# Placing all matrix operands of a two-block network at one place modulo 256 bytes

## The chip, the cores and the metric

The kernel runs on one core of a Trainium2 chip. The metric is the device time of one execution in microseconds (us), as the median of several runs. Of one further execution the hardware profiler kept a trace; all rows below come from it.

## What is computed

The input is 256 rows of 1024 numbers in float32. Two blocks follow each other: `first_block` has two layers, `second_block` four SwiGLU feed-forward parts, one hybrid mixer and one recurrent mixer. Cut to the matrix products, which carry the work:

```python
def first_block(x, ...):                       # layers "first0", "first1"
    for l in range(2):
        h = rms_norm(x, norm_g[l])
        ... = split(h @ w_in[l])               # gmlp, retention, gated delta net (GDN)
        branches = stack([y_a, y_b, y_c])
        gates = sigmoid(einsum(h, w_gate[l]))
        x = x + sum(gates * einsum(branches, w_branch_out[l])) @ w_out[l]
    return rms_norm(x, final_norm_g)

def second_block(x, ...):                      # ffn00, hyb, ffn01, ffn10, rec, ffn11
    for layer in range(2):
        h = swiglu(rms_norm_2(x, g[0]), ffn_w_in[layer, 0], ffn_w_out[layer, 0])
        x = x + 0.5 * rms_norm_2(h, g[1])
        h = rms_norm_2(x, g[2])
        h = hybrid_mixer(h, ...) if layer == 0 else recurrent_mixer(h, ...)
        x = x + rms_norm_2(h, g[3])
        h = swiglu(rms_norm_2(x, g[4]), ffn_w_in[layer, 1], ffn_w_out[layer, 1])
        x = x + 0.5 * rms_norm_2(h, g[5])
    return x
```

## The kernel before

**Products in three passes.** Each float32 operand is split into a high part and a low part in the type fp32r (`split`: ScalarE casts, VectorE subtracts), and a product is the sum of high x high, high x low and low x high. The normalised rows stand transposed in `hh` and `hl`; the hidden values of a feed-forward part in `ah` and `al`; other left operands are `yh`/`yl`, `g2` (printed as `g`), `oh`/`ol`, `roh`/`rol`.

**Weight units.** `unit` fetches the next 128 x 1024 piece of the weight stream into `st` by a DMA and splits it into `wh` and `wl`. Six buffers of each lie in the pool `wp`. In the feed-forward parts and the recurrent mixer three more lie in the pool of the phase (`xp`); there, of each nine units that follow each other, six use the first pool and three the second.

**Three loops use the units.** A matmul has a stationary operand (128 x 128, loaded by LDWEIGHTS while the matmul ahead of it runs) and a moving operand. In a trace row `mm<-a,b`, a is the moving operand and b the stationary one.
- `ws`: the unit is stationary and `hh`/`hl` move (256 columns). A unit takes 24 matmuls, in the order `hh,wh`, `hl,wh`, `hh,wl`. There are 208 such units: 36 in each of the four feed-forward parts, 24 in the two layers of the first block, 28 in the hybrid mixer, 12 in the recurrent one.
- `xs` and `outp`: the unit moves (512 columns) and the left operand is stationary; a unit takes 12 matmuls. `outp` of a feed-forward part uses 22 units.

**Where operands lie.** A tile gets its address from the order and the sizes of the tiles in its pool. In the program as built, modulo 256 bytes: `hh`, `hl` and the units of `wp` start at 128; the units of `xp` at 192 in the feed-forward parts and at 160 in the recurrent mixer; `ah`/`al` and `g2` at 192, `oh`/`ol` at 64, `roh`/`rol` at 160, `yh`/`yl` at 0. Slices step by multiples of 512 bytes, so a whole tile has one place. Below, the **offset** of a pair is the place of the stationary operand that is loaded during a matmul, less the place of that matmul's moving operand, modulo 256. By the program, the `ws` matmuls stand so: offset 0 for 156 units (96 of them in the feed-forward parts), 64 for the 48 units of `xp` in the feed-forward parts, 32 for 4 units of the recurrent mixer. In `outp` of the feed-forward parts 60 units have offset 64 and 28 have 0; `outp` of the first block (`g2`, 16 units) has 64, that of the hybrid mixer (`oh`, 16 units) 192. The 24 units on `yh` have 128, some 8 on `roh` 32, the 8 on `hh` that use `xp` 192. All other `xs` units, on `hh`, have 0.

**Order.** Instructions of PE, DVE, ACT and the SP queue are put in order by a scheduler; POOL follows the program. `step` runs one piece of background work (GDN, retention, LRU, attention) between the parts of a loop.

Of the kernel before, what the change touches and what calls it, by code (L numbers as in the profile page):

```python
# [23 lines left out]
FX = 2  # L24

NW, NS = 6, 5

LO, LF, LH, LR = 4, 6, 4, 5

# [139 lines left out]
class Net:  # L169
# [36 lines left out]
        return self.ps.tile([128, 512], F32, tag="mm", name="mm", bufs=4)  # L206

    def t(self, tag, shape, dt=F32, bufs=1, pool=None):
        return (pool or self.ph).tile([128] + list(shape), dt, tag=tag, name=tag, bufs=bufs)

    def bcast(self, row, tag, c0=0, n=1024):
        t = self.t(tag, [n])
# [65 lines left out]
        self.nc.scalar.copy(hi, src)  # L278
        self.nc.vector.tensor_sub(lo, src, hi)  # L279

    def unit(self, g=None):

        if self.pre:
            return self.pre.popleft()
        st = self.wp.tile([128, 1024], F32, tag="st", name="st", bufs=NS)
        self.nc.sync.dma_start(st, self.a["wst"][self.wi])
        pool, n = self.wp, NW
        if self.ui % (NW + self.xn) >= NW:
            pool, n = self.xp, self.xn
        self.wi += 1  # L290
        self.ui += 1
        hi = pool.tile([128, 1024], F32R, tag="wh", name="wh", bufs=n)
        lo = pool.tile([128, 1024], F32R, tag="wl", name="wl", bufs=n)
        if g is None:
            self.split(hi, lo, st)
        else:
            for j in range(2):
                s = self.pn[:, g + j:g + j + 1]
                self.act(hi[:, CS[j]], st[:, CS[j]], AF.Copy, scale=s)
                self.stt(lo[:, CS[j]], st[:, CS[j]], s, hi[:, CS[j]], MUL, SUB)  # L300
        return hi, lo
# [57 lines left out]
    def ws(self, evac, pair=None):  # L359

        self.flush()
        hh, hl = self.hT
        ps = [self.mmt().rearrange("p (a b) -> p a b", a=2) for _ in range(2)]
        for k2 in range(4):
            wh, wl = (w.rearrange("p (a b) -> p a b", a=2) for w in self.unit(None if self.gn is None else self.gn + 2 * k2))
            for f in range(4):
                p = ps[f // 2][:, f % 2]  # L370
                fs = slice(f * 128, f * 128 + 128)
                for j in range(2):
                    k = k2 * 2 + j
                    self.mm(p, wh[:, j, fs], hh[:, :, k], start=k == 0 and f % 2 == 0, stop=False)
                    self.mm(p, wh[:, j, fs], hl[:, :, k], start=False, stop=False)
                    self.mm(p, wl[:, j, fs], hh[:, :, k], start=False, stop=k == 7 and f % 2 == 1)
                if f % 2:
                    if k2 == 3 and pair is not None:
                        pair(f // 2, ps[f // 2])
                    elif k2 == 3:  # L380
                        for e in (f - 1, f):
                            evac(e, ps[e // 2][:, e % 2])
                    self.step()
# [2 lines left out]
        hh, hl = self.hT  # L386
        return lambda k, t: (hh[:, t, k], hl[:, t, k])

    def small_proj(self, src, n, out):

        w = self.t("junk", [512], pool=self.sp)[:, :8 * n].rearrange("p (a b) -> p a b", a=8)
        self.nc.sync.dma_start(w, src.rearrange("p (a b) -> p a b", a=8))
        wh, wl = self.t("spwh", [8, n], F32R), self.t("spwl", [8, n], F32R)
        self.split(wh, wl, w)
        hh, hl = self.hT
        yield
        p = self.sm()[:n, :256]
        for k in range(8):
            self.mm(p, wh[:, k], hh[:, :, k], start=k == 0, stop=False)
            self.mm(p, wh[:, k], hl[:, :, k], start=False, stop=False)  # L400
            self.mm(p, wl[:, k], hh[:, :, k], start=False, stop=k == 7)
            if k % 2:
                yield
        o = self.t("junk", [512], pool=self.sp)[:, :256]
        self.nc.scalar.copy(o[:n], p)
        yield
        p = self.sm()[:, : 2 * n].rearrange("p (a b) -> p a b", a=2)
        for t in range(2):
            self.nc.tensor.transpose(p[:, t], o[:n, TS[t]], self.ident[:n, :n])
        out.append(p)  # L410
# [75 lines left out]
    def post(self, ph, half, prep, tag="h"):  # L486

        g = self.bcast(B_PN + POST[ph], "bcp")  # L490
        k = 4.0 if half else 1.0
        rs = self.rs

        tmps, vs = [None, None], [None, None]

        def cb(t, c, ps):
            if c == 0:
                tmps[t] = self.t(tag, [1024], bufs=2)
                vs[t] = self.t("rsv", [1], bufs=4, pool=self.sp)
            tmp, v = tmps[t], vs[t]  # L500
            ss = self.sumsq(ps, self.t("junk", [512], pool=self.sp))
            self.tt(tmp[:, CS[c]], ps, g[:, CS[c]])
            if c == 0:
                self.ts(v, ss, k / D, rs[t][:, 1:2] if half else EPS, MUL, ADD)
                return
            self.stt(v, ss, k / D, v, MUL, ADD)
            r = self.t("rsr", [1], bufs=4, pool=self.sp)
            self.pw(r, v)
            for c in range(2):
                x = self.x[t][:, CS[c]]  # L510
                self.stt(x, tmp[:, CS[c]], r, x, MUL, ADD)
            prep(t, tmp)

        return cb
# [26 lines left out]
    def run(self):  # L541
        tc, nc, a = self.tc, self.nc, self.a
        with (
# [22 lines left out]

            self.act(cp.tile([128, 1], F32, tag="first", name="first"), self.mhalf[:, :1], AF.Tanh)
            nc.sync.dma_start(self.x[0], a["x"][TS[0]])
            with tc.tile_pool(name="start", bufs=1) as self.ph:
                prep = self.prep_open(self.phases[0])  # L570
                nc.sync.dma_start(ci, a["ci"])
                nc.sync.dma_start(self.x[1], a["x"][TS[1]])

                z, warm = self.t("z", [128]), self.sm()
                nc.vector.memset(z, 0.0)
                for n in range(WARM):
                    self.mm(warm[:, :128], z, z, start=True, stop=True)
                self.ui = self.xn = 0
                for t in range(2):
                    prep(t, self.t("h", [1024], bufs=2))  # L580
                    if t == 0 and self.phases[0].startswith("first"):
                        first = [self.unit() for _ in range(3)]
                self.pre.extend(first)
# [3 lines left out]
            for p in order:  # L587
                i = self.phases.index(p) + 1
                nxt = self.phases[i] if i < len(self.phases) else None
                self.hT, self.rs = self.next  # L590
                self.gn = PN.get(p)
                self.ui = 0
                self.xn = 0 if p.startswith("first") or p == "hyb" else 3
                with tc.tile_pool(name=p, bufs=1) as self.ph:
                    self.xp = self.ph if self.xn else None
                    if p.startswith("first"):
                        self.first(int(p[5]), nxt)
                    elif p.startswith("ffn"):
                        self.ffn(p, nxt)
                    elif p == "hyb":  # L600
                        self.hyb(nxt)
                    elif p == "rec":
                        self.rec(nxt)
                    self.flush()
# [345 lines left out]
    def gdn_ab(self, l, G):  # L950
        nc = self.nc
        ab = []
        yield from self.small_proj(self.a["sw"][:, S_AB + l * 128:S_AB + (l + 1) * 128], 16, ab)
        ab = ab[0]
        sv = self.sv[:, l * V_L:(l + 1) * V_L]
        ar = self.t("gar", [8])
        self.act(ar, sv[:, 8:16], AF.Exp)
        xa = self.t("gxa", [2, 2, 4])
        be = self.t("gbe", [2, 2, 4])
        for t in range(2):  # L960
            a4 = ab[:, t].rearrange("p (d w h) -> p d w h", d=2, w=2)
            self.tt(xa[:, t], a4[:, :, 0], sv[:, 16:24].rearrange("p (d h) -> p d h", d=2), ADD)
            self.act(be[:, t], a4[:, :, 1], AF.Tanh, scale=0.5)
        xf = xa.rearrange("p t d h -> p (t d h)")
        g = self.t("gg", [2, 2, 4])
        gf = g.rearrange("p t d h -> p (t d h)")
        self.softplus(gf, xf, [16], "gs")
        for t in range(2):
            gt = g[:, t].rearrange("p d h -> p (d h)")
            self.stt(gt, gt, -1.0, ar)  # L970
        bf = be.rearrange("p t d h -> p (t d h)")
        nc.vector.tensor_scalar(bf, bf, 0.5, 0.5, op0=MUL, op1=ADD)
        G.update(g=g, be=be)

    def gdn_core(self, G):
# [87 lines left out]
        ea, eb = [ex[:, 0], ex[:, 2]], [ex[:, 1], ex[:, 3]]  # L1063
        for _ in range(5):
            yield
        tx = self.t("gtx", [256])[:64]
        for j in range(1, 31):
            n = 31 - j
            u = tx[:, :n * j].rearrange("p (a b) -> p a b", a=n)
# [155 lines left out]
    def hyb(self, nxt):  # L1225
# [29 lines left out]
        def gate(g):  # L1255

            def cz(t, ps):
                th = self.silu2(ps, "h2", 5)
                yv = y[t][:, g * 8:g * 8 + 8].rearrange("p a b -> p (a b)")
                self.tt(yv, yv, th)  # L1260
                junk = self.t("junk", [512], pool=self.sp)
                r = self.rstd(self.sumsq(yv, junk), 1.0 / 512, 4 * EPS)
                self.stt(yv, yv, r, gb[:, CS[g]])
                ks = slice(4 + g * 8, 8 + g * 8)
# [293 lines left out]
```

## Time and profile before

| what | value |
|---|---|
| median of 3 runs | 1722.13 us (1720.92 to 1723.18) |
| profiled execution, its own time | 1723.59 us |
| its span in the trace | 1721.6 us |
| mean granted TensorE clock | 0.992 |
| PE busy (share of the span) | 1690.0 us (98%) |
| DVE, ACT, POOL busy | 1193.8, 883.7, 154.3 us |

The span is the time from the first to the last instruction in the trace; 2.0 us of the execution's time lie around it. A matmul's busy time is longer than the distance to the next one, since matmuls are pipelined: the distance between starts (the pitch) is what a matmul costs.

### The profile page before, as it was taken

The page shows a single profiled execution, that of the slowest core. Times are in us where ns is not written, and L with a number is a line of the kernel's source. Part 1 is how long each engine was busy: PE and PEld are TensorE (multiplying, and loading weights), DVE is VectorE, ACT ScalarE, POOL GpSimd, SP SyncE. Part 2 cuts the span into 40 slices and gives each one's busy share as a digit, 9 for nine tenths or more (in the row PEclk, how much of TensorE's full clock was granted, in tenths as well). Part 3 has the DMA queues.
Part 4 walks back from the last instruction along what each step waited for, and adds up shares of the span by engine and source line. Part 5 has one row for each costly group of instructions (what it writes and reads, how often), then busy time and mean ns, then how long its engine had stood idle before and what let it go on. Part 6 is the DMA issues. An engine that isn't in the chain of part 4 may idle for free.

```text
span 1721.6 us, 26744 instructions
## 1 busy us (share of the span) xinstructions
PE 1690.0 (98%) x10312; PEld 1493.2 (87%) x10312; DVE 1193.8 (69%) x1941; ACT 883.7 (51%) x1387; POOL 154.3 (9%) x205
## 2 busy tenths in 40 slices
PE   9999999999999999999999999999999999999998
PEld 8888888798878888998798887999789987879986
DVE  6888666679855658764678767775586637987743
ACT  5553344554523447553554556653475435875532
POOL 0157000004630000000000000000000000000000
PEclk9999999999989999999999999999999999999999
DMA  8546435554553447554454335754565545446542
GB/s 292 171 163 208 135 105 195 175 175 154 171 171 111 160 156 257 186 184 149 164 171 156 106 128 195 237 185 149 177 242 187 184 151 201 162 150 227 178 156 73
DMA packets 83279, 296.80 MB, mean 172 GB/s; under 512 B 9680, under 2 KB 10320, under 8 KB 83152
## 3 DMA queue, kind: packets, MB, share of 16 engines
q1 hardware_dynamic: 81360, 289.85, 51.0%
q0 software_dynamic: 1792, 5.24, 1.1%
q8 instruction: 81, 1.33, 0.3%
q14 instruction: 46, 0.38, 0.1%
HBM read 290.33 MB, written 4.72 MB: 171 GB/s over the span
## 4 chain that ended last, share of the span: by engine, by line
PE 81%; DVE 7%; POOL 4%; ACT 3%; DMA 2%; issue 2%; SPq 0%; POOLq 0%; DVEq 0%; ACTq 0%
PE mm L199 71%; PE gd L199 6%; PE sm L199 2%; PE sm L274 2%; DVE wl L279 2%; POOL rsr L417 1%; POOL gtx L1070 1%; POOL gv L1072 1%; DMA st<-in_wst_dram 1%; DVE wl L193 1%; ACT wh L278 1%; PE gd L274 1%; DVE x L193 1%; DVE ro L190 1%; ACT wh L196 1%
## 5 line engine op out<-in xcount | busy, mean ns | idle before, releaser
L279 DVE TENSOR_TENSOR wl<-st,wh 128x1024 fp32r<-128x1024 f32 x348 | 429.2, 1241 | 278.6 <-ACT wh L278 277.5
L278 ACT CAST wh<-st 128x1024 fp32r<-128x1024 f32 x348 | 364.0, 1049 | 439.5 <-PE mm L199 402.4
L199 PE MATMUL mm<-hh,wh 128*128 128x256 f32 x1664 | 474.9, 285 | 0.0
L199 PE MATMUL mm<-hl,wh 128*128 128x256 f32 x1664 | 471.9, 284 | 0.0
L199 PE MATMUL mm<-hh,wl 128*128 128x256 f32 x1664 | 471.2, 283 | 0.0
L199 PEld LDWEIGHTS mm<-hh,wh 128*128 128x128 f32 x1664 | 318.9, 192 | 2.4 <-issue 1.7
L199 PEld LDWEIGHTS mm<-hl,wh 128*128 128x128 f32 x1664 | 317.4, 191 | 2.1 <-issue 1.7
L199 PEld LDWEIGHTS mm<-hh,wl 128*128 128x128 f32 x1664 | 317.4, 191 | 1.2 <-issue 1.0
L193 DVE SCALAR_TENSOR_TENSOR wl<-st,ci,wh 128x512 fp32r<-128x512 f32 x352 | 251.3, 748 | 77.5 <-ACT wh L196 77.5
L196 ACT ACTIVATE wh<-st,ci 128x512 fp32r<-128x512 f32 x352 | 233.9, 715 | 105.2 <-PE mm L199 81.1
L199 PE MATMUL mm<-wh,hh 128*128 128x512 f32 x656 | 267.8, 410 | 2.3 <-ACT wh L278 2.3
L199 PE MATMUL mm<-wh,hl 128*128 128x512 f32 x656 | 260.4, 397 | 0.0
L199 PE MATMUL mm<-wl,hh 128*128 128x512 f32 x656 | 259.0, 396 | 0.0
L199 PEld LDWEIGHTS mm<-wh,hh 128*128 128x128 f32 x656 | 124.9, 190 | 26.6 <-ACT wh L278 2.5
L199 PEld LDWEIGHTS mm<-wh,hl 128*128 128x128 f32 x656 | 124.5, 190 | 26.7 <-issue 0.5
L199 PEld LDWEIGHTS mm<-wl,hh 128*128 128x128 f32 x656 | 124.9, 190 | 24.2 <-issue 0.5
L199 PE MATMUL mm<-wl,ah 128*128 128x512 f32 x352 | 138.9, 394 | 0.0
L199 PE MATMUL mm<-wh,ah 128*128 128x512 f32 x352 | 138.4, 393 | 0.0
L199 PE MATMUL mm<-wh,al 128*128 128x512 f32 x352 | 138.3, 393 | 0.0
L417 POOL TENSOR_TENSOR rsr<-rsv,mhalf 128x1 f32<-128x1 f32 (+1 forms) x32 | 28.9, 902 | 1207.9 <-DVE rsv L193 940.0
L199 PEld LDWEIGHTS mm<-wh,ah 128*128 128x128 f32 x352 | 65.9, 187 | 15.8
L199 PEld LDWEIGHTS mm<-wh,al 128*128 128x128 f32 x352 | 65.9, 187 | 15.6
(385 smaller groups left out, 2019.6 us busy)
## 6 DMA issues: line engine op xcount, KB each, us to landing
st<-in_wst_dram SPq DMA_DIRECT2D x524, 512.0 KB, 4.0
bcp<-in_bc_dram SPq DMA_DIRECT2D x7, 512.0 KB, 5.4
gdl<-g POOLq DMA_DIRECT2D x8, 256.0 KB, 2.7
cst<-in_bc_dram SPq DMA_DIRECT2D x4, 512.0 KB, 5.2
g<-gdt POOLq DMA_DIRECT2D x8, 256.0 KB, 4.4
bcn<-in_bc_dram SPq DMA_DIRECT2D x3, 512.0 KB, 5.2
x<-in_x_dram SPq DMA_DIRECT2D x2, 512.0 KB, 4.8
cst<-in_cst_dram SPq DMA_DIRECT2D x4, 256.0 KB, 4.1
```

Source lines behind the costliest of these rows:

```text
L190: self.nc.vector.tensor_scalar(o, a, s1, s2, op0=op0, op1=op1)
L193: self.nc.vector.scalar_tensor_tensor(o, a, s, b, op0=op0, op1=op1)
L196: self.nc.scalar.activation(o, i, f, **k)
L199: self.nc.tensor.matmul(*a, **k)
L274: self.nc.tensor.transpose(p[:, j], s, self.ident)
L278: self.nc.scalar.copy(hi, src)
L279: self.nc.vector.tensor_sub(lo, src, hi)
L417: self.nc.gpsimd.tensor_tensor(o, i, self.mhalf[:, :i.free_size()], op=ALU.pow)
L1070: nc.gpsimd.tensor_tensor(u, X[:, j + 1:, j:j + 1].to_broadcast([64, n, j]), X[:, j:j + 1, :j].to_broadcast([64, n, j]), op=MUL)
L1072: nc.gpsimd.tensor_tensor(X[:, j + 1:, :j], X[:, j + 1:, :j], u, op=SUB)
```

## The change

Four things are done. `unit` allocates one tile of 2112 elements, which holds the high part and, 4096 bytes further, the low part, and takes an offset for each: `ws` asks for 16 and 48 elements (64 and 192 bytes), the other loops for none. Small tiles, whose size isn't a multiple of 256 bytes, go to a pool of their own (`phs`) behind that of the phase, and `junk` is lengthened, so that all tiles of the other pools start at the same place. `small_proj` keeps its split weights for GDN in the buffers of `yh`/`yl` (two of each) and not in `spwh`/`spwl`, and the POOL solve of GDN keeps its products `tx` in one of the two `ggm` buffers and not in `gtx`.

```diff
+WS = 16, 48
...
     def t(self, tag, shape, dt=F32, bufs=1, pool=None):
-        return (pool or self.ph).tile([128] + list(shape), dt, tag=tag, name=tag, bufs=bufs)
+        pool = pool or (self.phs if math.prod(shape) % 64 else self.ph)
+        return pool.tile([128] + list(shape), dt, tag=tag, name=tag, bufs=bufs)
...
-    def unit(self, g=None):
+    def unit(self, g=None, off=(0, 0)):
...
-        hi = pool.tile([128, 1024], F32R, tag="wh", name="wh", bufs=n)
-        lo = pool.tile([128, 1024], F32R, tag="wl", name="wl", bufs=n)
+        w = pool.tile([128, 2112], F32R, tag="wh", name="wh", bufs=n)
+        hi, lo = (w[:, a + o:a + o + 1024] for a, o in zip((0, 1024), off))
...
-            wh, wl = (w.rearrange("p (a b) -> p a b", a=2) for w in self.unit(None if self.gn is None else self.gn + 2 * k2))
+            wh, wl = (w.rearrange("p (a b) -> p a b", a=2) for w in self.unit(None if self.gn is None else self.gn + 2 * k2, WS))
...
-        wh, wl = self.t("spwh", [8, n], F32R), self.t("spwl", [8, n], F32R)
+        wh, wl = (self.t(g, [512], F32R, bufs)[:, :8 * n].rearrange("p (a b) -> p a b", a=8) for g in tags)
...
-        yield from self.small_proj(self.a["sw"][:, S_AB + l * 128:S_AB + (l + 1) * 128], 16, ab)
+        yield from self.small_proj(self.a["sw"][:, S_AB + l * 128:S_AB + (l + 1) * 128], 16, ab, ("yh", "yl"), 2)
...
-        tx = self.t("gtx", [256])[:64]
+        tx = self.t("ggm", [256], bufs=2)[:64]
```

In the program as built, `hh`, `hl`, `ah`, `al`, `g2`, `yh`, `oh`, `roh` and the units of `xs` and `outp` then start at 128 modulo 256, so that all their matmuls have offset 0 but seven. In `ws` the high part starts at 192 (offset 64) and the low part at 64 (offset 192). The order `hh,wh`, `hl,wh`, `hh,wl` makes that offsets 64, 192, 64: during `hh,wh` the same high part is loaded anew, during `hl,wh` the low part, during `hh,wl` the next high part. Every engine runs the same instructions as before, and each feed-forward part in the same order; the order differs in places of the other phases.

One place is on DVE in `first0`, where units of `ws` are subtracted while GDN's gates (`gxa`, `gsu`, `gss`) are computed; names of semaphores that an instruction waits for stand in brackets. Before:

```order
L184 TENSOR_TENSOR gxa<-sm,sv 128x8 [waits Activation_49]
L193 SCALAR_TENSOR_TENSOR gsu<-gxa 128x16 [waits DVE_49]
L279 TENSOR_TENSOR wl<-st,wh 128x1024 [waits DMAHW2_49,PE_49,Activation_49]
L193 SCALAR_TENSOR_TENSOR g_266<-mm,pp,g_266 128x255 [waits Activation_49]
L188 TENSOR_SCALAR gss<-gsu 128x16 [waits Activation_49]
```

And of the change, at the same place on DVE:

```order
L186 TENSOR_TENSOR gxa<-sm,sv 128x8 [waits Activation_49]
L195 SCALAR_TENSOR_TENSOR g_270<-mm,pp,g_270 128x255 [waits Activation_49]
L195 SCALAR_TENSOR_TENSOR gsu<-gxa 128x16 [waits DVE_49]
L195 SCALAR_TENSOR_TENSOR g_270<-mm,pp,g_270 128x255 [waits DVE_49]
L283 TENSOR_TENSOR wh<-st,wh 128x1024 [waits DMAHW2_49,Activation_49]
```

The subtraction no longer waits for PE itself, only for the cast, since the cast ahead of it now writes into a tile that both parts share and waits until PE has read both; the low part is now printed as `wh` too.

The other place is on PE in `rec`, where the last `ws` matmuls end, `outp` begins (`mm<-wh,roh`) and the last two gate matmuls of the LRU (`rx,wa` and `rx,wx`) stand between them. Before:

```order
L199 MATMUL mm<-hh,wh 128x256
L199 MATMUL mm<-hl,wh 128x256
L199 MATMUL mm<-hh,wl 128x256
L199 MATMUL mm<-wh,roh 128x512
L199 MATMUL mm<-wl,roh 128x512
L199 MATMUL mm<-wh,rol 128x512
L199 MATMUL gd<-rx_14238,wa 128x256
L199 MATMUL gd<-rx_14238,wx 128x256
L199 MATMUL mm<-wh,roh 128x512
```

And of the change:

```order
L201 MATMUL mm<-hh,wh 128x256 x2
L201 MATMUL mm<-hl,wh 128x256
L201 MATMUL gd<-rx_13831,wa 128x256
L201 MATMUL gd<-rx_13831,wx 128x256
L201 MATMUL mm<-hh,wh 128x256
L201 MATMUL mm<-wh,roh 128x512 x2
L201 MATMUL mm<-wh,rol 128x512
```

The two gate matmuls have moved from behind the first three matmuls of `outp` to ahead of them.

## Rows read from the trace of the kernel before

**Rows 1.** The page: span, and PE's busy time with its share and instructions.

```profile
span 1721.6 us, 26744 instructions
...
PE 1690.0 (98%) x10312; PEld 1493.2 (87%) x10312; DVE 1193.8 (69%) x1941; ACT 883.7 (51%) x1387; POOL 154.3 (9%) x205
```

**Rows 2.** The page: the chain that ended last, by engine.

```profile
PE 81%; DVE 7%; POOL 4%; ACT 3%; DMA 2%; issue 2%; SPq 0%; POOLq 0%; DVEq 0%; ACTq 0%
```

**Rows 3.** Waits of PE: for what, us in total, times, longest.

```profile
PE gd L199 <- DVE g L1100: 7.7, 3, 3.7
...
PE mm L199 <- ACT roh L278: 2.8, 1, 2.8
PE mm L199 <- ACT wh L278: 2.3, 1, 2.3
```

**Rows 4.** The page's groups: count, busy us, mean ns of one, idle before.

```profile
L199 PE MATMUL mm<-hh,wh 128*128 128x256 f32 x1664 | 474.9, 285 | 0.0
...
L193 DVE SCALAR_TENSOR_TENSOR wl<-st,ci,wh 128x512 fp32r<-128x512 f32 x352 | 251.3, 748 | 77.5 <-ACT wh L196 77.5
L196 ACT ACTIVATE wh<-st,ci 128x512 fp32r<-128x512 f32 x352 | 233.9, 715 | 105.2 <-PE mm L199 81.1
...
L199 PE MATMUL mm<-wl,ah 128*128 128x512 f32 x352 | 138.9, 394 | 0.0
```

**Rows 5.** Timeline of PE, ffn00, first `ws` unit (`xp`): start us, us.

```profile
673.96 0.61 PE L199 MATMUL sm<-rdg,cst 128*128 128x128 f32 x4
...
674.76 0.28 PE L199 MATMUL mm<-hh,wh 128*128 128x256 f32 x1
...
676.91 0.28 PE L199 MATMUL mm<-hl,wh 128*128 128x256 f32 x1
```

**Rows 6.** Timeline of PE, the next six `ws` units (`wp`).

```profile
677.14 0.38 PE L274 MATMUL sm<-ci,sg 128*128 128x128 f32 x2
...
677.84 0.28 PE L199 MATMUL mm<-hl,wh 128*128 128x256 f32 x1
...
693.92 0.28 PE L199 MATMUL mm<-hh,wh 128*128 128x256 f32 x1
```

**Rows 7.** Timeline of PE, the three `ws` units behind them (`xp`).

```profile
694.75 0.28 PE L199 MATMUL mm<-hl,wh 128*128 128x256 f32 x1
...
702.76 0.28 PE L199 MATMUL mm<-hh,wh 128*128 128x256 f32 x1
```

**Rows 8.** Timeline of PE, `xs` on `hh` in first0, offset 0.

```profile
127.75 0.39 PE L199 MATMUL mm<-wh,hh 128*128 128x512 f32 x1
...
136.82 0.39 PE L199 MATMUL mm<-wl,hh 128*128 128x512 f32 x1
```

**Rows 9.** Timeline of PE, `outp` of ffn00, units at offset 64.

```profile
779.65 0.39 PE L199 MATMUL mm<-wh,ah 128*128 128x512 f32 x1
...
786.89 0.39 PE L199 MATMUL mm<-wl,ah 128*128 128x512 f32 x1
```

**Rows 10.** Timeline of PE, `outp` of the hybrid mixer, offset 192.

```profile
1032.79 0.39 PE L199 MATMUL mm<-wh,oh 128*128 128x512 f32 x1
...
1043.77 0.39 PE L199 MATMUL mm<-wh,oh 128*128 128x512 f32 x1
```

**Rows 11.** Timeline of PE, `ws` of the recurrent mixer, offset 32.

```profile
1464.76 0.28 PE L199 MATMUL mm<-hh,wl 128*128 128x256 f32 x1
...
1468.90 0.28 PE L199 MATMUL mm<-hl,wh 128*128 128x256 f32 x1
```

**Rows 12.** Waits of ACT: the cast of a unit.

```profile
ACT wh L278 <- PE mm L199: 402.4, 227, 8.8
```

**Rows 13.** Timeline of PE, the last gate matmuls of the LRU.

```profile
1497.77 0.59 PE L199 MATMUL gd<-rx,wa 128*128 128x256 f32 x2
```

**Rows 14.** Tile `ggm` in first0 (first and last start), and POOL's first product.

```profile
L199 PE MATMUL gd<-ggm,cst x8: 591/592/676, 66.6 to 82.4; 128*128 128x512 f32 x8
...
98.59 0.35 POOL L1070 TENSOR_TENSOR gtx<-gv 64x30 f32<-64x30 f32 x1 [3.51 <-DMA gv<-gdl]
```

More of the change, by code (lines that the diff above doesn't have):

```diff
@@ L387, in hlhs, with small_proj @@
         return lambda k, t: (hh[:, t, k], hl[:, t, k])
-    def small_proj(self, src, n, out):
-        w = self.t("junk", [512], pool=self.sp)[:, :8 * n].rearrange("p (a b) -> p a b", a=8)
+    def small_proj(self, src, n, out, tags=("spwh", "spwl"), bufs=1):
+        w = self.t("junk", [560], pool=self.sp)[:, :512][:, :8 * n].rearrange("p (a b) -> p a b", a=8)
         self.nc.sync.dma_start(w, src.rearrange("p (a b) -> p a b", a=8))
-        wh, wl = self.t("spwh", [8, n], F32R), self.t("spwl", [8, n], F32R)
+        wh, wl = (self.t(g, [512], F32R, bufs)[:, :8 * n].rearrange("p (a b) -> p a b", a=8) for g in tags)
         self.split(wh, wl, w)
@@ L403, in small_proj @@
                 yield
-        o = self.t("junk", [512], pool=self.sp)[:, :256]
+        o = self.t("junk", [560], pool=self.sp)[:, :512][:, :256]
         self.nc.scalar.copy(o[:n], p)
@@ L500, in cb @@
             tmp, v = tmps[t], vs[t]
-            ss = self.sumsq(ps, self.t("junk", [512], pool=self.sp))
+            ss = self.sumsq(ps, self.t("junk", [560], pool=self.sp)[:, :512])
             self.tt(tmp[:, CS[c]], ps, g[:, CS[c]])
@@ L568, in run @@
             nc.sync.dma_start(self.x[0], a["x"][TS[0]])
-            with tc.tile_pool(name="start", bufs=1) as self.ph:
+            with tc.tile_pool(name="start", bufs=1) as self.ph, tc.tile_pool(name="starts", bufs=1) as self.phs:
                 prep = self.prep_open(self.phases[0])
@@ L593, in run @@
                 self.xn = 0 if p.startswith("first") or p == "hyb" else 3
-                with tc.tile_pool(name=p, bufs=1) as self.ph:
+                with tc.tile_pool(name=p, bufs=1) as self.ph, tc.tile_pool(name=p + "s", bufs=1) as self.phs:
                     self.xp = self.ph if self.xn else None
@@ L1260, in cz @@
                 self.tt(yv, yv, th)
-                junk = self.t("junk", [512], pool=self.sp)
+                junk = self.t("junk", [560], pool=self.sp)[:, :512]
                 r = self.rstd(self.sumsq(yv, junk), 1.0 / 512, 4 * EPS)
```

## The prediction

> **What bounds the kernel now.** I read the page first: PE is busy for 1690.0 of 1721.6 us, 98% [rows 1], and the chain that ended last is 81% PE, with 7% DVE and 4% POOL [rows 2]. Then the waits of PE: the largest is 7.7 us in three pieces for GDN's `g`, then 2.8 us once for `roh` and 2.3 us once for a `wh` [rows 3]. So almost nothing is late for PE, and time can come only from matmuls that follow each other faster. The groups give no cost per matmul: 285 ns is the mean busy time of an `hh,wh` and 394 ns that of a `wl,ah` [rows 4], but matmuls overlap. So I went to the timeline and took distances between starts, over long stretches without a break.
>
> The reader should see two things there. First, one `ws` loop runs at three speeds. The first unit of ffn00 lies in `xp` (offset 64) and takes (676.91 − 674.76)/19 steps = 113.2 ns per matmul [rows 5]; the next six lie in `wp` (offset 0): (693.92 − 677.84)/134 = 120.0 ns [rows 6]; the three behind them, again in `xp`: (702.76 − 694.75)/68 = 117.8 ns [rows 7]. Instructions, sizes and left operand are the same, only the unit's place differs. Second, 512 columns want the opposite: offset 0 gives (136.82 − 127.75)/40 = 226.8 ns [rows 8], offset 64 (786.89 − 779.65)/31 = 233.5 [rows 9], offset 192 (1043.77 − 1032.79)/48 = 228.8 [rows 10]. Offset 32 in `ws` gives (1468.90 − 1464.76)/35 = 118.3 [rows 11].
>
> Offset 64 has two values in `ws`, and [rows 5, 7] differ in what came ahead: the 113.2 follows short float32 matmuls (`sm<-rdg,cst` at 673.96), the 117.8 a stretch at 120.0. My reading, an argument and no row: at offset 0 each load collides with the running stream at once and the pair stays locked in a late order; at 64 a late order heals in part, and an order that starts well is kept. The fast value also ends in ffn00 when `sm<-ci,sg` [rows 6] breaks in, but the units behind it have offset 0, so the rows don't say whether a break alone ends it.
>
> **The change part by part.** The sum is made against the profiled execution's 1723.59 us; the median of 1722.13 is 1.46 lower.
>
> (1) `ws` of the feed-forward parts at offset 0: 96 units × 24 = 2304 matmuls at 120.0. They get offsets 64, 192, 64. The trace has no `ws` matmul at 192; bounds are the best and the worst that `ws` shows, 113.2 and 120.0 [rows 5, 6]. I take 113.2 for both offsets: with no stretch at offset 0 left, a part enters its loop as in [rows 5], behind short matmuls, and nothing is left in it that would disturb the good state. 2304 × 6.8 ns = 15.7 us.
>
> (2) `ws` of the feed-forward parts at 64 already: 48 × 24 = 1152 matmuls. Some 23 in each of the four parts run at 113.2 now (those of [rows 5] and the like in the other parts), so 1152 − 92 = 1060 go from 117.8 to 113.2: 1060 × 4.6 = 4.9 us.
>
> (3) The other `ws` matmuls: 60 units at 0 (1440) and 4 at 32 (96). Short matmuls of the background stand between them, so that the state may be lost and found; I take the middle of both values at 64, 115.5: 1440 × 4.5 + 96 × 2.8 = 6.8 us.
>
> (4) 512 columns, all to offset 0 and 226.8. `outp` of the feed-forward parts: 60 units × 12 = 720 × 6.7 (233.5 less 226.8) = 4.8 us; the 28 at offset 0 already count nothing. `g2`: 16 × 12 = 192 × 6.7 = 1.3. `oh`: 192 × 2.0 = 0.4. For `yh` (288, offset 128), `roh` (96) and the 96 on `hh` that use `xp` no row was counted, so they lie between 0 and 480 × 6.7 = 3.2 us; I take 1.2, under the middle, since offset 192 costs only 2.0 [rows 10]. Together 7.7.
>
> (5) The shared tile, counted at nothing. The cast now waits until PE has read both halves. In `ws` the last matmul of a unit reads the low part, so the cast is released one step later (0.12 us); in the other loops the last one reads the high part as it is, and nothing changes. Behind the cast on ACT stand other casts and the copies that free PSUM for PE. It is hidden because casts already wait 402.4 us in 227 waits for PE to free buffers [rows 12], six units ahead of use: DVE needs 2 × 748 and ACT 2 × 715 ns for a unit [rows 4] where PE takes 24 × 113.2 = 2717 ns in `ws` and 12 × 226.8 = 2722 in the others, so both finish with over a microsecond to spare after PE gets faster. With that cover gone it would cost up to 208 × 0.12 = 25 us.
>
> (6) `tx` in `ggm`, nothing: POOL's first product stands at 98.59, the last matmul that reads `ggm` starts at 82.4 [rows 14], 16 us ahead. The buffers of `yh`/`yl` for `small_proj` are equally far from use: their product comes in the first stretch of a layer, `yh` at its end.
>
> (7) The new order in `first0` and in `rec`, nothing: DVE does the same work. The two gate matmuls (0.59 us, [rows 13]) now stand ahead of the first `outp` matmuls, where PE waits 2.8 us for `roh` [rows 3]; if they fall into that wait up to 0.6 us is won. GDN's 7.7 us hangs on DVE and POOL; a PE that comes there sooner would wait longer. But the stretch ahead of it is `xs` at offset 0 [rows 8], which gains nothing, so I move neither.
>
> Sum: 15.7 + 4.9 + 6.8 + 7.7 = 35.1 us, so 1723.59 − 35.1 = 1688.5, and **1687 us** as a median.
>
> **The rivals.** "0.2%" is 3.4 us, about what a measurement of this kernel can tell from no change.
>
> A. *Offset 64 settles at 117.8.* There are 68 steps of it without a way back [rows 7], and only 19 of the good state; short matmuls inside the loop could break it. Then (1) is 2304 × 2.2 = 5.1, (2) is 92 × −4.6 = −0.4, (3) is 1440 × 2.2 + 96 × 0.5 = 3.2, with (4) 15.6: 1708.0 in the profile, 1706.5 as a median. Should the third of the steps that load at 192 also run at 120.0, the mean is 118.5, the gain 3.5 − 1.2 + 2.1 + 7.7 = 12.1, and the median 1710.
>
> B. *Only the load at 192 collides.* 64, 192 and 64 make 113.2, 120.0, 113.2, a mean of 115.5. (1) 2304 × 4.5 = 10.4, (2) 1060 × 2.3 − 92 × 2.3 = 2.2, (3) by a mean of 117.0, 1440 × 3.0 + 96 × 1.3 = 4.4, (4) 7.7: 24.7, median 1697. For it: no row shows `ws` at 192, and the nearest other offset, 32, has 118.3 [rows 11]. Against: 32 stands nearer to 0, and what 512 columns dislike (64 most, 192 a little, [rows 9, 10]) has so far been good for `ws`.
>
> C. *Slower: the background becomes late.* PE gets through `ws` 4 to 6% sooner, while the chains of the background on DVE, ACT and POOL keep their length; where one of them fills a phase (hybrid and recurrent mixer), PE then waits at each step of it. The three waits for GDN show the price: 7.7/3 = 2.6 us each [rows 3], and a lower clock behind them: the mean granted clock of 0.992 in the table above is 0.008 × 1721.6 = 13.8 us of full speed lost, 4.6 for each wait if all of it hangs on them. At 7.2 us apiece it decides from (35.1 + 3.4)/7.2, that is six such waits more: 8 us slower, 1730. Against it: PE waits for hardly anything else now [rows 3], and two thirds of the gain lies in the feed-forward parts, which have no background of that kind.
>
> D. *The place is not what divides the 120.0 from the 117.8*, but the phase in which the stream was entered, as [rows 5, 7] differ at one offset: then nothing happens, 1722 ± 2. Against it: the three values change exactly where the pools change, and 512 columns follow their offsets in other phases too. [...]
>
> **How the numbers follow.** Forecast 0.46: the mechanism shows in every row above, the state's endurance doesn't. A 0.25 (a third of it with the slow load at 192); B 0.19; C 0.05; D 0.05. The low end has all `ws` at 113.2 and all bounds of (4): (3) grows by 1440 × 2.3 + 96 × 2.3 = 3.5, (4) by 2.0, (7) by 0.6: 41.2, so 1681, and 1680 with rounding; the high end is A's worse half, 1710, and 1711. Faster is forecast, A and B: 0.90; same is D, 0.05; slower is C, 0.05.
>
> **What would show it.** Starts of `ws` matmuls in ffn00 113.2 ns apart throughout, and the mean busy time of `hh,wh` down from 285 by some 5 ns; (1) and (2) fall if 117.8 or more is found, B holds if only the step of `hl,wh` (the load at 192) is long. `outp` on `ah` at 226.8 and `wl,ah` below 394 show (4). PE's wait for `wh` staying at a few us shows (5). It would be wrong in kind if pitches don't follow offsets, or if PE's waits grow past some 20 us.

## The result, and the profile after

The changed kernel takes 1692.56 us (median of 4 runs, 1691.46 to 1693.84) where the kernel before takes 1722.66: a ratio of 0.9826, 95% interval 0.9811 to 0.9842, 30.1 us less. The forecast was 1687 with a range of 1680 to 1711.

The page of the changed kernel, its span, its busy engines and the chain that ended last, beside [rows 1, 2]:

```profile
span 1691.7 us, 26739 instructions
...
PE 1656.2 (98%) x10312; PEld 1467.1 (87%) x10312; DVE 1195.0 (71%) x1941; ACT 884.1 (52%) x1387; POOL 156.6 (9%) x205
...
PE 83%; DVE 6%; POOL 4%; ACT 3%; issue 2%; DMA 2%; SPq 0%; POOLq 0%; DVEq 0%; ACTq 0%
```

The same 10312 matmuls keep PE busy for 33.8 us less, and the span is 29.9 us shorter; DVE, ACT and POOL did the same work in nearly the same time. PE is as much the bound as before. Its groups, with count, busy us, mean ns and idle time, beside [rows 4] (both halves of a unit are now printed as `wh`), and the cast of a unit:

```profile
L201 PE MATMUL mm<-hh,wh 128*128 128x256 f32 x3328 | 584.6, 279 | 0.0
L282 ACT CAST wh<-st 128x1024 fp32r<-128x1024 f32 x348 | 364.3, 1051 | 401.1 <-PE mm L201 363.8
L201 PE MATMUL mm<-hl,wh 128*128 128x256 f32 x1664 | 461.1, 277 | 0.0
L201 PE MATMUL mm<-wh,al 128*128 128x512 f32 x352 | 137.0, 389 | 0.0
```

In the kernel before, the page had for two of these groups

```profile
L199 PE MATMUL mm<-hl,wh 128*128 128x256 f32 x1664 | 471.9, 284 | 0.0
...
L199 PE MATMUL mm<-wh,al 128*128 128x512 f32 x352 | 138.3, 393 | 0.0
```

A mean busy time tells only that something fell (284 to 277 for `hl,wh`, 393 to 389 for `wh,al`). The size is in the starts. Two marks of the timeline in ffn00, one step of each third being `hl,wh`, and two of `outp` on `al`:

```profile
672.21 0.28 PE L201 MATMUL mm<-hl,wh 128*128 128x256 f32 x1
...
758.91 0.28 PE L201 MATMUL mm<-hl,wh 128*128 128x256 f32 x1
...
767.44 0.39 PE L201 MATMUL mm<-wh,al 128*128 128x512 f32 x1
...
822.52 0.39 PE L201 MATMUL mm<-wh,al 128*128 128x512 f32 x1
```

765 steps lie between the first two: 113.3 ns each, over nearly the whole of the loop, where [rows 6, 7] had 120.0 and 117.8. 243 steps lie between the last two: 226.7 ns, where [rows 9] had 233.5. The waits of PE (us, times, longest), beside [rows 3]:

```profile
PE gd L201 <- DVE g L1106: 6.9, 3, 3.5
PE sm L278 <- DVE h L195: 6.1, 5, 2.9
PE sm L278 <- DVE x L195: 2.6, 6, 0.6
PE mm L201 <- ACT wh L282: 2.2, 1, 2.2
PE mm L201 <- ACT roh L282: 2.2, 1, 2.2
PE sm L278 <- DVE sg L195: 1.7, 4, 0.7
...
PE gd L201 <- DVE rx L195: 1.4, 2, 1.2
```

The wait for a `wh` is as short as before, so the shared tile costs PE next to nothing. New is `rx`, and `x` had 1.9 before; for `h` and `sg` the kernel before had

```profile
PE sm L274 <- DVE h L193: 4.6, 4, 2.9
...
PE sm L274 <- DVE sg L193: 0.8, 3, 0.5
```

To see where 30 us come from, all distances between starts of PE in the trace were added up: what a `ws` step takes over 113.2 ns and a 512-column step over 226.8 ns at full clock (a granted clock of 1.00; single steps that are over 40 ns late stand apart, 28 us in both kernels), what a step takes longer when a short float32 matmul comes behind it, and the time of the steps at the lower clock (a granted clock of 0.50, as from 495 to 505 us in the kernel before and from 179 to 187 us in the changed one; in the kernel before, the five 512-column steps from 497.77 us on take 426 ns each).

| us in all | before | changed | changed, second profile |
|---|---|---|---|
| `ws` over 113.2 ns | 29.8 | 2.1 | 1.9 |
| 512 columns over 226.8 ns | 12.0 | 2.9 | 2.9 |
| longer ahead of short float32 matmuls | 26.0 | 30.7 | 29.2 |
| steps at the lower clock | 22.6 (74 steps) | 26.8 (85) | 23.3 (69) |

The first two lines are a gain of 27.7 + 9.1 = 36.8 us. The third gives 4.7 back. The fourth gives 4.2 back, of which some 3.0 are work that stands at full clock in the trace of the kernel before; 1.2 are lost. The last column is from the kernel run again, below: the lower clock differs from one execution to the next, the third line less so.

### The profile page after: what moved, and what is told of

The parts are those of the page before. It is cut to its first block, busy times and chain, and to the rows that moved or that the text cites. A ratio compares the mean times of both kernels' runs of the same rounds, so it can differ in the third digit from the quotient of the medians.

```text
span 1691.7 us, 26739 instructions
## 1 busy us (share of the span) xinstructions
PE 1656.2 (98%) x10312; PEld 1467.1 (87%) x10312; DVE 1195.0 (71%) x1941; ACT 884.1 (52%) x1387; POOL 156.6 (9%) x205
## 4 chain that ended last, share of the span: by engine, by line
PE 83%; DVE 6%; POOL 4%; ACT 3%; issue 2%; DMA 2%; SPq 0%; POOLq 0%; DVEq 0%; ACTq 0%
PE mm L201 72%; PE gd L201 6%; PE sm L278 2%; PE sm L201 2%; DVE wh L283 2%; POOL rsr L423 1%; POOL ggm L1076 1%; POOL gv L1078 1%; PE gd L278 1%; ACT wh L282 1%; DMA st<-in_wst_dram 1%; DVE ro L192 1%; DVE wh L195 1%; DMA g<-gdt 1%; DVE x L195 0%
## 5 line engine op out<-in xcount | busy, mean ns | idle before, releaser
L283 DVE TENSOR_TENSOR wh<-st,wh 128x1024 fp32r<-128x1024 f32 x348 | 429.1, 1241 | 261.0 <-ACT wh L282 260.2
L201 PE MATMUL mm<-hh,wh 128*128 128x256 f32 x3328 | 584.6, 279 | 0.0
L282 ACT CAST wh<-st 128x1024 fp32r<-128x1024 f32 x348 | 364.3, 1051 | 401.1 <-PE mm L201 363.8
L201 PEld LDWEIGHTS mm<-hh,wh 128*128 128x128 f32 x3328 | 506.4, 188 | 3.4 <-issue 2.4
L201 PE MATMUL mm<-wh,hh 128*128 128x512 f32 x1312 | 426.1, 404 | 2.7 <-ACT wh L282 2.2
L195 DVE SCALAR_TENSOR_TENSOR wh<-st,ci,wh 128x512 fp32r<-128x512 f32 x352 | 251.3, 747 | 62.1 <-ACT wh L198 61.9
L201 PEld LDWEIGHTS mm<-wh,hh 128*128 128x128 f32 x1312 | 243.5, 191 | 51.4 <-ACT wh L282 2.4
L201 PE MATMUL mm<-wh,ah 128*128 128x512 f32 x704 | 217.5, 390 | 0.0
L201 PEld LDWEIGHTS mm<-wh,ah 128*128 128x128 f32 x704 | 131.8, 188 | 27.1
L201 PE MATMUL mm<-wh,yh 128*128 128x512 f32 x192 | 60.9, 398 | 0.0
L1076 POOL TENSOR_TENSOR ggm<-gv 64x30 f32<-64x30 f32 (+14 forms) x60 | 49.3, 821 | 11.1 <-DMA gv<-gdl 7.0
```

The lines of the kernel that those rows point to most:

```text
L195: self.nc.vector.scalar_tensor_tensor(o, a, s, b, op0=op0, op1=op1)
L201: self.nc.tensor.matmul(*a, **k)
L1076: nc.gpsimd.tensor_tensor(u, X[:, j + 1:, j:j + 1].to_broadcast([64, n, j]), X[:, j:j + 1, :j].to_broadcast([64, n, j]), op=MUL)
```

## The experiments

**The place alone.** All of the change stays, only the offsets of `ws` go.

```diff
-WS = 16, 48
+WS = 0, 0
```

> The changed kernel with WS = 0, 0: everything else of the change stays (one tile for both halves, the pool for small tiles, the left operands and moving units at one place), only the ws units lie at offset 0 again, all of them. Theory of the place: the ws matmuls go back to 120.0 ns, 4948 x 6.8 ns = 33.6 us more than the changed kernel's 1692.6, so about 1726 us, less up to 5 us if the longer waits and the lower clock of the changed kernel come from its faster PE and vanish with it: 1720 to 1727. Rival, the rest of the layout (one buffer for both halves, fewer waits on DVE, another order) gave the time: stays within 3 us of 1692.6. The 512-column matmuls stay near 226.8 in both.

Two marks in ffn00, 708 steps apart:

```profile
683.68 0.28 PE L201 MATMUL mm<-hl,wh 128*128 128x256 f32 x1
...
768.64 0.28 PE L201 MATMUL mm<-hl,wh 128*128 128x256 f32 x1
```

That is 120.0 ns again. Measured: 1717.35 us, ratio to the kernel before on the same chip 0.9965 (0.9953 to 0.9977). The added-up starts show 32.9 us over 113.2 in `ws` (all of its units now at 120.0), and 3.0 in 512 columns. So the rest of the change is worth 0.35%, about 6 us: 9.0 for 512 columns, less 3.1 since the `ws` units of `xp` lost their offset too. The places of the `ws` units are worth the difference of the two ratios, 1.4%, some 24 us. The rival falls. The time is 3 us under the range that I gave: of the 30.8 us that `ws` loses in its steps, about 6 come back elsewhere, more than the 5 that I allowed: 3.1 ahead of short matmuls (27.6 where the first profile of the changed kernel has 30.7; its second has 29.2), some 2 since 11 steps fewer stand at the lower clock (23.0 us, not 26.8).

**Which offsets.** Each feed-forward part gets another place for both halves.

```diff
+WP = {"ffn00": (16, 16), "ffn01": (48, 48), "ffn10": (32, 32), "ffn11": (8, 8)}
...
-            wh, wl = (w.rearrange("p (a b) -> p a b", a=2) for w in self.unit(None if self.gn is None else self.gn + 2 * k2, WS))
+            wh, wl = (w.rearrange("p (a b) -> p a b", a=2) for w in self.unit(None if self.gn is None else self.gn + 2 * k2, WP.get(self.part, WS)))
```

> The changed kernel, with another place for both halves of the ws units in each feed-forward part: all loads at offset 64 in ffn00, 192 in ffn01, 128 in ffn10, 32 in ffn11. Theory of the place, with a collision at offset 0 only: 64, 192 and 128 all run at 113.2 ns, and 32, which is nearer to 0, at 113 to 118 (118.3 in the recurrent mixer of before). Rival, it takes the alternation of 64 and 192 (neighbouring loads at different places): the uniform parts run at 117 to 120. Rival B of the prediction (192 collides by itself): ffn01 at 120.

Marks of the timeline in ffn00 (offset 64), ffn01 (192), ffn10 (128):

```profile
679.45 0.28 PE L202 MATMUL mm<-hl,wh 128*128 128x256 f32 x1
...
766.02 0.28 PE L202 MATMUL mm<-hl,wh 128*128 128x256 f32 x1
...
1083.37 0.28 PE L202 MATMUL mm<-hl,wh 128*128 128x256 f32 x1
...
1169.93 0.28 PE L202 MATMUL mm<-hl,wh 128*128 128x256 f32 x1
...
1271.36 0.28 PE L202 MATMUL mm<-hl,wh 128*128 128x256 f32 x1
...
1357.87 0.28 PE L202 MATMUL mm<-hl,wh 128*128 128x256 f32 x1
```

735, 735 and 729 steps: 117.8, 117.8 and 118.7 ns; ffn11 (32) has 118.3 over 717. A single run took 1706.72 us. My theory fell here, and rival B's 120 for offset 192 didn't come either. No single place gave 113.3 in this run, and ffn00 with 64 alone, entered from the same `sm<-rdg,cst` as the changed kernel, runs at 117.8 from its first unit on. From this entry the 113.3 of the changed kernel needs both places; the entry test below shows that 64 alone can reach it from another.

**512 columns.** The left operands of `outp` are moved.

```diff
+AO = {"ffn00": 16, "ffn01": 48, "ffn10": 32, "ffn11": 8}
...
+    def left(self, tag, ph, n):
+        o = AO[ph]
+        return self.t(tag, [2 * n + 64], F32R)[:, o:o + 2 * n].rearrange("p (a b) -> p a b", a=2)
```

> The changed kernel, with the left operands ah and al of outp moved by 64 bytes in ffn00, 192 in ffn01, 128 in ffn10 and 32 in ffn11 (their tiles are 256 bytes longer). Theory of the place: 512-column matmuls take 233.5, 228.8, about 232 and about 233 ns in the four parts in place of 226.8, together 264 x (6.7 + 2.0 + 5 + 6) ns = 5.2 us more. Rival, the pitch of outp in the kernel before came from the two pools between which its units changed, not from the offset: 226.8 in all four.

Marks in ffn00 (64) and ffn01 (192):

```profile
763.65 0.40 PE L202 MATMUL mm<-wh,al 128*128 128x512 f32 x1
...
820.35 0.39 PE L202 MATMUL mm<-wh,al 128*128 128x512 f32 x1
...
1165.16 0.40 PE L202 MATMUL mm<-wh,al 128*128 128x512 f32 x1
...
1217.35 0.40 PE L202 MATMUL mm<-wh,al 128*128 128x512 f32 x1
```

243 steps at 233.3 and 228 at 228.9 ns; 128 gives 232.4 (243 steps, ffn10) and 32 gives 233.3 (213 steps, ffn11). The added-up 512 columns rise from 2.9 to 8.4 us, 5.5 more, where 5.2 was expected. The rival of the two pools falls. The one time, 1691.49 us, doesn't show it, because this profile has only 41 steps at the lower clock (13.5 us) where the changed kernel has 85, and stands 1.6 us less ahead of short matmuls: a single time can't weigh 5 us here, and the pitch can.

That it is the offset and not the left operand's own place is in the trace of the kernel before. There `ah` and `al` lie at 192 throughout, and behind the 233.5 of [rows 9], with units at 128, come units at 192:

```profile
788.51 0.39 PE L199 MATMUL mm<-wh,al 128*128 128x512 f32 x1
...
789.87 0.39 PE L199 MATMUL mm<-wh,al 128*128 128x512 f32 x1
```

6 steps, 226.7 ns. For 256 columns no run separates the two: `hh` and `hl` stood at 128 in all of them.

**One bad unit.** A single unit at offset 0 in each feed-forward part.

```diff
+BAD = ("ffn00", 0), ("ffn01", 2), ("ffn10", 2), ("ffn11", 2)
...
+        if (p, n) in BAD:
+            return 0, 0
+        return (16, 16) if p == "ffn10" else WS
...
+            if self.part == "ffn11" and self.wn == 19:
+                q = self.sm()[:, :128]
+                self.mm(q, self.ONE, self.ident, start=True, stop=True)
```

> The changed kernel, with one ws unit (24 matmuls) at offset 0 in each feed-forward part: the first unit in ffn00 (short float32 matmuls stand behind it), the third in the other parts; in ffn10 all other units at 64 and 64, and in ffn11 one short float32 matmul put in front of unit 19. Theory of the kept state (the prediction's reading): the bad unit runs at 120.0, and what follows it keeps 117.8 in ffn01 and ffn10 to the end of the loop; in ffn00 the short matmuls bring back 113.2, and in ffn11 it is 117.8 up to unit 19 and 113.2 from there. Some 2 x 33 x 24 x 4.6 ns = 7 us and 2 us in all. Rival, no state: only the bad unit's 24 matmuls are slow (0.16 us each), 113.2 at once behind it, and the 117.8 of before came from something else.

Marks in ffn01: the bad unit (18 steps of it), then 738 steps behind it. The last two are in ffn10, with 64 alone, 738 steps behind its bad unit:

```profile
1071.68 0.28 PE L202 MATMUL mm<-hl,wh 128*128 128x256 f32 x1
...
1073.84 0.28 PE L202 MATMUL mm<-hl,wh 128*128 128x256 f32 x1
...
1075.23 0.28 PE L202 MATMUL mm<-hl,wh 128*128 128x256 f32 x1
...
1158.87 0.28 PE L202 MATMUL mm<-hl,wh 128*128 128x256 f32 x1
...
1259.76 0.28 PE L202 MATMUL mm<-hl,wh 128*128 128x256 f32 x1
...
1346.68 0.28 PE L202 MATMUL mm<-hl,wh 128*128 128x256 f32 x1
```

The one run took 1695.48 us. 120.0 ns in the bad unit, and at once 113.3 behind it in ffn01 (the whole next unit has a mean of 114.0), in ffn11 too, where the short matmul therefore had nothing to mend. In ffn10 it is 117.8, but it was so ahead of the bad unit as well. So 64 and 192 in turn come back to the good order by themselves; nothing of the bad unit is kept.

**Other pairs.**

```diff
+WP = {"ffn00": (48, 16), "ffn01": (16, 32), "ffn10": (0, 48), "ffn11": (8, 56)}
```

> The changed kernel, with another pair of offsets (high part, low part) of the ws units in each feed-forward part: 192 and 64 in ffn00, 64 and 128 in ffn01, 0 and 192 in ffn10, 32 and 224 in ffn11. The earlier scan gave 117.8 ns for 64 alone and for 192 alone, where the changed kernel's 64 and 192 in turn give 113.3. Theory of the balance (two places that lie as far ahead of the moving operand as behind it lead back to the good order from any entry): 113.3 in ffn00 and ffn11, 117 to 120 in ffn01 and ffn10. Rival, any two different places do it: 113.3 in ffn01 as well, and in ffn10 too if 0 is no exception. Second rival, only 64 and 192 do: ffn11 at 117 to 120 also.

In ffn00 the two halves overlap, so that the last 32 of a high part's 1024 columns hold numbers of the low part; the instructions are the same. Marks in ffn00:

```profile
679.16 0.28 PE L202 MATMUL mm<-hl,wh 128*128 128x256 f32 x1
...
765.83 0.28 PE L202 MATMUL mm<-hl,wh 128*128 128x256 f32 x1
```

729 steps: 118.9 ns, with the two offsets of the changed kernel exchanged (the run took 1706.79 us). The other pairs give 118.2 (64 and 128, 735 steps), 117.8 (0 and 192, 735) and 118.2 (32 and 224, 717). The theory of the balance falls with ffn00 and ffn11, the rival of any two places with all of them. What is left is narrower than all three: of the pairs tried only 64 for the high part and 192 for the low one gives 113.3. That the pair with 0 at two steps of three is no worse than the others, 117.8, I had not expected either.

**The entry.** Offset 64 alone, and a short matmul in front of the seventh unit.

```diff
+EO = {"ffn00": 16, "ffn01": 0, "ffn10": 48, "ffn11": 32}
...
+            if self.part in EO and self.wn == 7:
+                q, o = self.sm()[:, :128], EO[self.part]
+                self.mm(q, self.ONE, self.ex[:, o:o + 128], start=True, stop=True)
```

> The changed kernel with both halves of the ws units at offset 64 in the feed-forward parts (117.8 ns in the earlier scan), and in front of the seventh ws unit of each part one short float32 matmul whose moving operand lies so that the load behind it is at offset 0 in ffn00, 64 in ffn01, 128 in ffn10 and 192 in ffn11. In the kernel before, the stretch at 113.2 [rows 5] was entered from short matmuls with a load at offset 0, the stretches at 117.8 were not. Theory of two orders that keep themselves, of which the entry chooses one: ffn00 runs at 113.2 from the seventh unit to its end (30 units x 24 x 4.6 ns = 3.3 us less), the others at 117.8 or also at 113.2, each in one of the two values throughout. Rival: every entry leads to 117.8, and the 113.2 of rows 5 came from the distance of 12288 bytes between the two halves, which this kernel doesn't have.

ffn00: 87 steps ahead of the short matmul, the short matmul, and 657 steps behind it:

```profile
671.88 0.28 PE L202 MATMUL mm<-hl,wh 128*128 128x256 f32 x1
...
682.13 0.28 PE L202 MATMUL mm<-hl,wh 128*128 128x256 f32 x1
...
682.72 0.39 PE L202 MATMUL sm<-ex,cst 128*128 128x128 f32 x2
...
684.09 0.28 PE L202 MATMUL mm<-hl,wh 128*128 128x256 f32 x1
...
758.55 0.28 PE L202 MATMUL mm<-hl,wh 128*128 128x256 f32 x1
```

117.8 ns ahead, 113.3 behind, with nothing between but one short matmul. The run took 1693.88 us. So at offset 64 there are two orders that keep themselves for hundreds of steps (735 at 117.8 ns in ffn00 of the scan, 657 at 113.3 here), and the entry chooses; the rival with the distance of 12288 bytes falls. The good order was entered with a load at offset 0, as in the four parts of the kernel before [rows 5]. Entries with a load at 64 went both ways: `sm<-rdg,cst` led to 117.8 in all four parts here, `sm<-ci,sg` in front of the second unit left ffn00 there, and brought the other three to 113.3, in which they stayed behind the short matmul whatever its place. In the two earlier runs with 64 alone (ffn00 of the scan, ffn10 of the bad unit) `sm<-ci,sg` led to 117.8. So those three parts don't tell what its place does, and that the place of the load turned ffn00, and not the break as such, rests on one case and on the entries of the kernel before.

**The same entry at other offsets.** The part of the entry test that worked, a load at offset 0 behind the short matmul, in all four parts, with 192 and 64 in turn (ffn00), and 192, 128 and 32 alone.

```diff
-EO = {"ffn00": 16, "ffn01": 0, "ffn10": 48, "ffn11": 32}
+EO = {"ffn00": 48, "ffn01": 48, "ffn10": 32, "ffn11": 8}
+WP = {"ffn00": (48, 16), "ffn01": (48, 48), "ffn10": (32, 32), "ffn11": (8, 8)}
```

> The kernel of the entry test once more, with other places of the ws units in the feed-forward parts: 192 and 64 in turn in ffn00 (118.9 before), 192 alone in ffn01 (117.8), 128 in ffn10 (118.7), 32 in ffn11 (118.3); the short matmul in front of the seventh unit lies so that the load behind it has offset 0 in all four, the entry that led offset 64 from 117.8 to 113.3. Theory of two orders at any offset but 0: all four run at 113.3 behind it. Rival, 64 is special (alone it has two orders, and only 64 with 192 in the third place leads to the fast one): no change at the seventh unit in ffn00, ffn01, ffn10 and ffn11. Where some change and others don't, the offsets with two orders are those that change.

The halves overlap in ffn00 as said above. Marks in ffn00, 72 steps ahead of the short matmul and 609 behind it:

```profile
672.94 0.28 PE L203 MATMUL mm<-hl,wh 128*128 128x256 f32 x1
...
681.50 0.28 PE L203 MATMUL mm<-hl,wh 128*128 128x256 f32 x1
...
686.35 0.28 PE L203 MATMUL mm<-hl,wh 128*128 128x256 f32 x1
...
758.76 0.28 PE L203 MATMUL mm<-hl,wh 128*128 128x256 f32 x1
```

118.9 ns on both sides; and behind the short matmul 117.8 (558 steps), 118.7 (561) and 118.3 (504) in the other three, as before it. The run took 1708.68 us. 64 is special so far: of the offsets tried, it alone is seen to have the second, faster order, while five entries each at 192, 128 and 32 (two in the scan, three here) all led to the slower one.

**What was given back.** Pieces of background work are held for a number of steps before their matmul is issued. Steps have become shorter (113.3 ns in ffn00, where 120.0 and 117.8 stood), DVE's busy time hasn't (1195.0 us, 1193.8 before).

```diff
-    def hold(self, fn, n=3):
+    def hold(self, fn, n=4):
```

> The changed kernel with transposes of background pieces held for 4 steps of a loop in place of 3 (where no number of steps is given). The changed kernel's PE stands 4.7 us longer ahead of short float32 matmuls than that of before. Theory of the count of steps: steps are shorter now, so a held piece comes before DVE has finished it; with one step more the waits for sg, h and rx go back by 1 to 3 us, and the time goes to 1690 to 1692. Rival, those waits stand at ends of phases, where nothing is left to put in front, and don't depend on the count: 1692 to 1694, the same waits.

1689.01 us (1687.76 to 1690.53), ratio 0.9796 (0.9774 to 0.9817), a little under the range that I gave. The time ahead of short matmuls fell from 30.7 to 28.2; the wait for `rx` stayed at 1.4. As this was 3.5 us better than the changed kernel on another chip, four kernels were put beside each other on one:

> The changed kernel as it is, to stand on one chip beside the three that follow: 1691 to 1694 us. A second profile also shows how much of its 4.7 us of longer stands ahead of short matmuls and of its lower clock belongs to the kernel and how much to the one execution that was profiled: if to the kernel, 29 to 31 us stand there again (26.0 in the kernel before).

> The changed kernel with held pieces at 4 steps, now beside the changed kernel on one chip. If the gain seen before (1689.0) is one of the kernel: 2 to 4 us under the changed kernel's median, and the wait for sg at or under 0.7 us. Rival: the 3.5 us were a difference of chips and rounds, and both agree within 1 us.

> The changed kernel with held pieces at 5 steps. If waits of held pieces are what is left there, another 0 to 1 us less than with 4; rival, the pieces now come late in their phase and what hangs on them waits at its end: 1 to 3 us more than with 4.

> The kernel before the change with held pieces at 4 steps. Theory that the shorter steps of the changed kernel brought the waits: here steps are long, sg waits only 0.8 us in all, so within 1 us of the kernel before (1722 to 1724). Rival, the longer hold is good by itself, whatever the pitch: 2 to 4 us less here too, and then it says nothing on what the change gave back.

| kernel | median us | ratio to before | 95% interval | ahead of short matmuls, us |
|---|---|---|---|---|
| changed | 1691.01 | 0.9810 | 0.9795 to 0.9825 | 29.2 |
| changed, held 4 | 1687.48 | 0.9790 | 0.9777 to 0.9803 | 28.3 |
| changed, held 5 | 1690.32 | 0.9808 | 0.9794 to 0.9821 | 27.8 |
| before, held 4 | 1722.54 | 0.9995 | 0.9986 to 1.0004 | 25.0 |

Waits for `sg` with the changed kernel run again, and with 4:

```profile
PE sm L278 <- DVE sg L195: 0.4, 1, 0.4
...
PE sm L278 <- DVE sg L195: 0.3, 1, 0.3
```

Held 4 is 3.5 us under the changed kernel both times, the intervals overlap both times, and in the kernel before the same edit moves the time by less than 1 us. So that a hold of 4 helps where steps are short, by some 3 us, is likely by the medians and not shown. A hold of 5 is 2.8 us above that of 4, as its rival has it, again with intervals that overlap. Why is not shown either: in the second profile `sg` waits only 0.4 us without the edit, the time ahead of short matmuls fell by 0.9 us and not by 3, and with 5 it falls further while the time goes back. Held 4 has the lowest median of all versions, 1687.48 us.

## Why the prediction was right, and where not

The number came out because the three terms of `ws`, 15.7 + 4.9 + 6.8 = 27.4, were measured at 27.7, and the fourth, 7.7, at 9.1. Inside the 27.7 two misses nearly cancel: by the same adding up, the feed-forward parts gave 19.8 where (1) and (2) have 20.6, and the other parts 7.8 where (3) has 6.8, since their `ws` steps settle at 113.3 too and not at the middle, 115.5. Rivals A, in both its forms, and B didn't happen. Rival D falls: one unit at offset 0 in the middle of a loop at 113.3 runs at 120.0.

**The step that failed in its reason is (1).** It took 113.2 because "a part enters its loop as in [rows 5]" and nothing in it disturbs the good order. Half of that holds: at offset 64 a good order, once entered, is kept (657 steps). But the entry isn't good by itself. In the kernel before, the load behind `sm<-rdg,cst` had offset 0; in the changed one it has 64, and with 64 alone such a part begins at 117.8, in all six parts of three kernels that had it. What carried the forecast is what the sum gave no credit to, that 64 and 192 in turn have one order only: all eight entries of the four feed-forward parts of the changed kernel, and two stretches behind a bad unit, end at 113.3 to 113.4 within a dozen steps. So (1) was right in its number by a way that it didn't name, and that was luck. Had both halves been put at 64, rival A would have been right in part, by what the entries happened to choose.

**The term that was left at nothing and wasn't is (7), with rival C behind it.** C was set aside since PE waited "for hardly anything else". It came at a small size: 4.7 us more ahead of short matmuls in this profile (3.2 in the second), on `h`, `x`, `sg` and `rx`, chains of DVE that didn't get shorter. With the lower clock (4.2 us more, 1.2 of them lost) and about a microsecond in the short matmuls themselves, that is why 36.8 us of faster steps became 30. The forecast of 35.1 had no such line. How much of the third line the shorter pitch causes is not settled: the kernel with offset 0, one profile of it, has 27.6, which lies between the 26.0 of the kernel before and the 30.7 and 29.2 of the changed one, and those two differ by 1.5 though the kernel is the same.

(5) and (6) hold: casts still wait 363.8 us for PE, 402.4 in [rows 12], the wait for `wh` is 2.2 us, and GDN's 7.7 became 6.9. For `roh` PE waits 2.2 in place of 2.8, as the upper bound of (7) has it.

Open: why 64, 192, 64 leads to the fast order and 192, 64, 192 does not, and by what an entry chooses at 64. No theory that I put up survived the pairs. What in the chip ties the pitch to the place, no run shows.

## What to carry to other kernels

When matmuls follow each other without a wait, measure the distance of their starts by the place of the next load against the moving operand, modulo 256 bytes: here it decides 6% of a 256-column step (113.3 or 120.0 ns) and 3% of a 512-column step (226.7 or 233.5), with the opposite choice for the two: of the offsets tried, 0 is the slowest in 256 columns (with the moving operand at 128 alone) and the fastest in 512. Take a layout from a kernel that was run, not from the best stretch of a trace, since that stretch may be one of two orders that its entry chose, as 113.3 and 117.8 ns at offset 64 here. And when steps get shorter, look again at every delay that is counted in steps: here that may be worth 3 us.

## What the runs showed that was not expected

At a granted clock of 1.00, four of the pitches have a common measure: 113.3, 120.0, 226.7 and 233.3 ns are 17, 18, 34 and 35 times 6.67 ns. Offset 64 and offset 192 alone, and the pair 0 and 192, all settle at 117.8, which is (113.3 + 120.0 + 120.0)/3 ns. At 64 that is no mix of steps at 113.3 and 120.0: each of the 68 steps of [rows 7] takes 117 to 119 ns. One short float32 matmul can change the speed of the next 657 matmuls by 4% (117.8 ns ahead of it and 113.3 behind it, in ffn00 of the entry test).
